# The first stage of a decoder block: small weights taken by halves, the first block of x ahead of the second, and one transfer moved to ScalarE's queue

## The chip, the cores and the metric

The kernel runs on one core of a Trainium2 chip. The metric is the device time of one execution in microseconds (us); the number given for a kernel is the median of its runs. A profile is one execution taken by the hardware profiler; its times count from the first instruction, and its span ends with the last.

Engines are named as the profile names them: PE (TensorE, matmuls), PEld (its weight loads), DVE (VectorE), ACT (ScalarE), POOL (GpSimd) and SP (SyncE, which here only issues DMAs). SPq and ACTq are the queues in which SP and ACT issue DMAs.

## The reference, cut to what matters

One layer on x of 512 tokens by 1024 channels, in float32. Only the first steps are touched by the change:

```python
hN = _rmsnorm(x, norm_g[l])          # x * rsqrt(mean(x*x) + eps) * g, per token
p = _split_in(hN @ w_in[l])          # one projection into all branches
...
vs = kvh(p["n_vs"])                  # selected and window values of the NSA branch
vw = kvh(p["n_vw"])
gates = jax.nn.sigmoid(p["n_g"] + b_nsa_gate[l])
...                                  # p["m_i"], p["m_f"]: input and forget gates of the mLSTM
```

Behind it come the two branches (a chunkwise mLSTM and a three-way sparse attention), their gates, two branch projections, a merge, an output projection, the residual and a last norm.

## The kernel before, in words

Every float32 product is made from two-part operands: a value is split into a high part (a rounded copy, written by ACT or POOL) and a low part (value minus high part, written by DVE), and a product is the sum of high x high, low x high and high x low. In the names, `h` at the end is a high part and `l` a low part: `hTh`, `hTl` for the normed and transposed x; `shi`, `slo` for the small weights; `wh`, `wl` for the others.

The first stage, which the change rewrites, takes the 512 tokens in four blocks of 128 (`xts[0]` to `xts[3]`, tile `xt`) and the 1024 channels in eight chunks `k` of 128. For each block `tb`:

- `stats(tb)`: ACT squares the block and sums it (`sq`; block 0 in two halves of 512 channels, the others in one piece), and POOL makes the factor `r` from the sum (`v`, then `r`).
- `normed(tb, hf)`: DVE multiplies one half of the channels by `r` and by the norm's weights, which lie in two PSUM banks.
- `turned(tb, hf, bank)`: four PE transposes into a PSUM bank; they need `ident`, the first 128 columns of `cst`.
- `high(tb, hf)` on ACT and `low(tb, hf)` on DVE write `hTh` and `hTl` from that bank; `whole(tb, hf)` on ACT keeps a plain copy in `gate` for later use.
- `some_of(tb, kind, ks)`: matmuls of 288 columns with the small weights (`w_small`: 288 columns of `w_in` for values and gates), `hh` = hTh x shi, `lh` = hTl x shi, `hl` = hTh x slo. A block needs 24 of them, 8 of each kind.
- `small_hi(k, eng)` and `small_lo(k)` split two chunks of the small weights, `raw` (tile `sraw`), into `shi` and `slo`. `raw` comes in two transfers of four chunks (576 KB each).
- `warm(n)`: n matmuls on zeros, which nothing uses.

All x blocks and both halves of `raw` come by SP's queue; the norm's weights and `ident` by ACT's.

In this stage ACT, DVE and PE run the instructions in the order in which the code names them (`tc.keep_in_program_order`), and POOL those under `keep(...)`. SP's DMAs are not kept: a scheduler places them. After `ordered.discard("pe")` the scheduler also places PE's work; there a stream of other weight products fills PE. A DMA on SP's queue also waits for an earlier one that used the same of eight semaphores (0 to 7).

After the first stage come the value, output-gate and gate-path products by a Strassen-like scheme (`winograd`), q and k, the attention, the mLSTM and the output projections. The change doesn't touch them.

Of the kernel before, what the change touches and what calls it, by code (L numbers as in the profile page):

```python
# [19 lines left out]
D = 1024  # L20
# [43 lines left out]
def build(  # L64
# [4 lines left out]
    nc = tc.nc  # L69
# [17 lines left out]
    keep = tc.keep_in_program_order  # L87
# [9 lines left out]
    def bank(tag, bufs):  # L97
        return psum.tile([128, 512], F32, name=tag, tag=tag, bufs=bufs)

    PP = lambda: bank("pp", 3)  # L100
# [4 lines left out]
    def f(ap):  # L105
        return ap.bitcast(F32)
# [181 lines left out]
    with tc.tile_pool(name="ph0", bufs=2, side="right") as p0, tc.tile_pool(  # L288
# [3 lines left out]
        xts = [p0.tile([128, D], F32, name="xt", tag="xt", bufs=4) for _ in range(NT)]  # L292
        raw = sp.tile([128, ND, SW], F32, name="sraw")

        grow = p0.tile([128, D], F32, name="grow", bufs=1)
        keep(nc.scalar.dma_start(grow[96:97, :], norm_g))
        act.preload_act_table_set("natural_log_exp_and_others")
        keep(nc.scalar.dma_start(cst[:, :CTRI], consts[:, :CTRI]))
        ordered.add("pe")
        zero = p0.tile([128, 384], F32R, name="zero", bufs=1)  # L300
# [4 lines left out]
        def warm(n):  # L305
            for _ in range(n):
                pe.matmul(idle[:, :256], zero[:, :128], zero[:, 128:], start=True, stop=True)

        warm(9)
        for hs in (slice(0, 512), slice(512, D)):  # L310
            nc.sync.dma_start(xts[0][:, hs], x[0, 0:128, hs])
        nc.sync.dma_start(xts[1], x[0, 128:256, :])
        for k in (0, 4):
            nc.sync.dma_start(raw[:, k : k + 4], w_small[:, k : k + 4])
        for tb in range(2, NT):
            nc.sync.dma_start(xts[tb], x[0, tb * 128 : (tb + 1) * 128, :])
        one = p0.tile([128, 128], F32, name="one", bufs=1)
# [10 lines left out]
        def small_hi(k, eng):  # L328
            ks = slice(k, k + 2)
            if eng == "a":  # L330
                A(shi[:, ks], raw[:, ks], AF.Copy)
            else:
                keep(pool.tensor_scalar(shi[:, ks], raw[:, ks], 1.0, 1.0, OP.mult, OP.mult))

        def small_lo(k):
            ks = slice(k, k + 2)
            dve.tensor_tensor(slo[:, ks], raw[:, ks], f(shi[:, ks]), OP.subtract)
# [4 lines left out]
        def squares(tb):  # L342
            sq = p0.tile([128, D], F32, name="sq", tag="sq", bufs=1)
            for n in range(1 if tb else 2):
                hs = slice(0, D) if tb else slice(n * 512, n * 512 + 512)
                part = ssq[:, NT * n + tb : NT * n + tb + 1]
                A(sq[:, hs], xts[tb][:, hs], AF.Square, accum_out=part, scale=D**-0.5)

        def factor(tb):
            v = p0.tile([128, 1], F32, name="v", tag="v", bufs=4)  # L350
            r = p0.tile([128, 1], F32, name="r", tag="r", bufs=4)
            rs.append(r)
            keep(pool.tensor_scalar(v, ssq[:, tb : tb + 1], EPS, None, OP.add))
            if tb == 0:
                keep(pool.tensor_tensor(v, v, ssq[:, NT : NT + 1], OP.add))
            keep(pool.tensor_tensor(r, v, mhalf[:, 0:1], OP.pow))

        def stats(tb):
            squares(tb)
            factor(tb)  # L360
# [16 lines left out]
        def normed(tb, hf):  # L377
            hs = slice(hf * 512, hf * 512 + 512)
            xv = xts[tb][:, hs]
            dve.scalar_tensor_tensor(xv, xv, rs[tb][:, 0:1], gB[hf], OP.mult, OP.mult)  # L380

        def turned(tb, hf, bank):
            for k in range(4):
                o = hf * 512 + k * 128
                pe.transpose(bank[:, k * 128 : (k + 1) * 128], xts[tb][:, o : o + 128], ident)
            banks[tb, hf] = bank.rearrange("p (k t) -> p k t", k=4)

        def high(tb, hf):
            A(hTh[:, hf * 4 : hf * 4 + 4, blk[tb]], banks[tb, hf], AF.Copy)

        def whole(tb, hf):
            q = gate[:, tb // 2 * 2 + hf].rearrange("p (k t) -> p k t", k=4)
            A(q[:, :, tb % 2 * 128 : tb % 2 * 128 + 128], banks[tb, hf], AF.Copy)

        def low(tb, hf):
            ks = slice(hf * 4, hf * 4 + 4)
            dve.tensor_tensor(
                hTl[:, ks, blk[tb]], banks[tb, hf], f(hTh[:, ks, blk[tb]]), OP.subtract
            )
# [3 lines left out]
        def some_of(tb, kind, ks, stop=False):  # L403
            ks = list(ks)
            start = tb not in sums
            if start:
                sums[tb] = PP()
            for k in ks:
                l = (hTl if kind == "lh" else hTh)[:, k, blk[tb]]
                r = (slo if kind == "hl" else shi)[:, k, :]  # L410
                pe.matmul(
                    sums[tb][:, :SW], l, r, start=start and k == ks[0], stop=stop and k == ks[-1]
                )

        lo4, hi4 = range(4), range(4, 8)
        stats(1)
        normed(0, 0)
        turned(0, 0, PT())
        warm(3)
        normed(0, 1)  # L420
        turned(0, 1, PT())
        small_hi(0, "p")
        high(0, 0)
        high(0, 1)
        small_hi(2, "a")
        warm(4)
        normed(1, 0)
        turned(1, 0, PP())
        some_of(0, "hh", lo4)
        normed(1, 1)  # L430
        turned(1, 1, idle)
        high(1, 0)
        small_hi(4, "a")
        high(1, 1)
        small_hi(6, "p")
        low(0, 0)
        small_lo(0)
        low(0, 1)
        small_lo(2)
        low(1, 0)  # L440
        low(1, 1)
        some_of(1, "hh", lo4)
        some_of(0, "lh", lo4)
        some_of(0, "hh", hi4)
        some_of(1, "hh", hi4)
        some_of(0, "lh", hi4)
        some_of(0, "hl", lo4)
        some_of(1, "hl", lo4)
        some_of(1, "lh", lo4)
        some_of(1, "lh", hi4)  # L450
        stats(2)
        whole(0, 0)
        whole(0, 1)
        stats(3)
        whole(1, 0)
        whole(1, 1)
        nc.sync.dma_start(bias, biases)
        vq = quarters(vview, ((0, 0), (1, 0)))
        normed(2, 0)
        turned(2, 0, PT())  # L460
        high(2, 0)
        small_lo(4)
        some_of(0, "hl", (4, 5))
        some_of(1, "hl", (4, 5))
        small_lo(6)
        some_of(0, "hl", (6, 7), stop=True)
        some_of(1, "hl", (6, 7), stop=True)
        normed(2, 1)
        turned(2, 1, PT())
        high(2, 1)  # L470
        some_of(2, "hh", lo4)
        normed(3, 0)
        turned(3, 0, idle)
        some_of(2, "hh", hi4)
        normed(3, 1)
        turned(3, 1, PS())
        low(2, 0)
        low(2, 1)
        evacuate(0, sums[0])
        for hf in range(2):  # L480
# [7 lines left out]
        for tb in (2, 3):  # L488
            if tb == 3:
                some_of(tb, "hh", lo4)  # L490
                some_of(tb, "hh", hi4)
            some_of(tb, "hl", lo4)
            some_of(tb, "hl", hi4)
            some_of(tb, "lh", lo4)
            some_of(tb, "lh", hi4, stop=True)
# [850 lines left out]
    for h in range(4):  # L1346
# [34 lines left out]
        for tb in range(NT):  # L1381
            po = PO() if tb == 2 else PT()
            for sb in range(tb + 1):
                a = KOFF[sb] + (tb - sb) * 128
                lh, ll = Sh[:, a : a + 128], Sl[:, a : a + 128]
# [307 lines left out]
```

## Time and profile before

| | us |
|---|---|
| median of 3 runs | 601.89 (601.44 to 602.06) |
| the profiled execution | 602.07 |
| its span, first to last instruction | 600.0 |
| PE busy | 590.8 (98%) |
| DVE, ACT, POOL busy | 484.9, 350.5, 81.1 |
| first stage on PE: start of the first transpose to the first matmul of the next stage | 7.52 to 26.19 |

PE is busy nearly throughout, so time is won or lost where PE stands still. A row of a timeline gives start, duration, engine, line, operation, output tile and input tile, shape, how often it stands in a row, and in brackets the idle time before it and what ended it. Line 80 is a helper through which all engines but POOL and SP record, so rows are told apart by their tiles.

### The profile page before, as it was taken

The numbers are of one execution on the slowest core, as the hardware profiler recorded it, in microseconds if no ns is written. First come the engines' busy times: TensorE is split into PE (matmuls) and PEld (weight loads), VectorE is DVE, ScalarE is ACT, GpSimd is POOL, SyncE is SP. The second block draws the span as 40 slices with busy tenths as digits, with TensorE's granted clock in tenths as the row PEclk, the third lists the DMA queues.
The fourth block names the chain that finished last, engine by engine and source line by source line (L and its number), as shares of the span: only waits on it lengthen the run. The fifth ranks groups of instructions, "written<-read, shape, count | busy, mean of one in ns | idle before, by whom it ended". The sixth has DMA issues, their size and how long they took to land.

```text
span 600.0 us, 8451 instructions
## 1 busy us (share of the span) xinstructions
PE 590.8 (98%) x2956; PEld 496.1 (83%) x2956; DVE 484.9 (81%) x901; ACT 350.5 (58%) x645; POOL 81.1 (14%) x136
## 2 busy tenths in 40 slices
PE   8999999999999999999999999999999999999995
PEld 6988888888888888888888888888888888888885
DVE  5899689597586889887977876889898979589975
ACT  6855546555447477566666765656566663424564
POOL 3000000000015013223323220001010101010121
PEclk9999999999999999999999999999999999999999
DMA  8946453502047663323133123422232236990733
GB/s 317 333 126 193 155 171 113 165 4 87 3 127 179 153 165 105 89 57 90 39 89 102 41 66 110 140 72 71 70 106 63 63 100 193 316 247 19 210 54 140
DMA packets 83573, 74.16 MB, mean 124 GB/s; under 512 B 3854, under 2 KB 65930, under 8 KB 83531
## 3 DMA queue, kind: packets, MB, share of 16 engines
q1 hardware_dynamic: 82232, 70.94, 39.3%
q0 software_dynamic: 1008, 2.36, 2.1%
q8 instruction: 23, 0.38, 0.3%
q10 hardware_dynamic: 290, 0.33, 0.2%
q14 instruction: 20, 0.16, 0.1%
HBM read 61.36 MB, written 8.45 MB: 116 GB/s over the span
## 4 chain that ended last, share of the span: by engine, by line
PE 79%; DVE 13%; ACT 3%; DMA 2%; issue 1%; POOL 1%; SPq 0%; POOLq 0%; ACTq 0%; DVEq 0%
PE pp L80 47%; PE ps L80 18%; PE pt L80 10%; DVE u L80 5%; PE po L80 4%; DVE wl L80 2%; ACT wh L80 1%; DMA xt<-x 1%; DVE qkl L80 1%; DVE num L80 1%; DVE xo L80 1%; POOL rho L1379 1%; ACT th L80 1%; DMA wr<-w_in 1%; ACT qkh L80 1%
## 5 line engine op out<-in xcount | busy, mean ns | idle before, releaser
L80 PE MATMUL pp<-hTl,wh 128*128 128x512 f32 x352 | 142.2, 404 | 0.0
L80 PE MATMUL pp<-hTh,wh 128*128 128x512 f32 x352 | 139.0, 395 | 0.0
L80 PE MATMUL pp<-hTh,wl 128*128 128x512 f32 x352 | 138.4, 393 | 0.0
L80 DVE TENSOR_TENSOR wl<-wr,wh 128x1024 fp32r<-128x1024 f32 x56 | 69.7, 1248 | 11.1 <-ACT wh L80 11.0
L80 PEld LDWEIGHTS pp<-hTh,wh 128*128 128x128 f32 x352 | 66.2, 188 | 12.8
L80 ACT ACTIVATE wh<-wr 128x1024 fp32r<-128x1024 f32 x56 | 58.3, 1058 | 30.3 <-PE pp L80 20.8
L80 PEld LDWEIGHTS pp<-hTh,wl 128*128 128x128 f32 x352 | 66.3, 188 | 10.6
L80 PEld LDWEIGHTS pp<-hTl,wh 128*128 128x128 f32 x352 | 66.3, 188 | 10.6
L80 ACT ACTIVATE P<-P,st 128x128 f32<-128x128 f32 (+3 forms) x64 | 35.7, 558 | 27.8 <-DVE st L80 27.7
L1123 POOL TENSOR_SCALAR P<-P,st 128x128 f32<-128x128 f32 (+3 forms) x56 | 37.8, 694 | 91.4 <-DVE st L80 59.4
L80 DVE TENSOR_TENSOR wl<-T,wh 128x1024 fp32r<-128x1024 f32 x28 | 34.1, 1223 | 14.5 <-ACT wh L80 14.4
L80 DVE TENSOR_TENSOR wl<-R,wh 128x1024 fp32r<-128x1024 f32 x28 | 33.8, 1220 | 10.2 <-ACT wh L80 10.1
L80 DVE TENSOR_TENSOR ptl<-pt,pth 128x512 fp32r<-128x512 f32 (+1 forms) x64 | 30.9, 485 | 11.3 <-ACT pth L80 10.6
L80 ACT ACTIVATE wh<-T 128x1024 fp32r<-128x1024 f32 x28 | 29.4, 1056 | 18.3 <-PE pp L80 11.0
L80 ACT ACTIVATE pth<-pt 128x512 fp32r<-128x512 f32 (+1 forms) x64 | 27.4, 428 | 20.4 <-PE pt L80 20.1
L80 ACT ACTIVATE wh<-R 128x1024 fp32r<-128x1024 f32 x28 | 29.1, 1056 | 12.4 <-PE pp L80 5.3
L80 DVE SCALAR_TENSOR_TENSOR u<-pp,prm,u 128x511 f32<-128x511 f32 (+2 forms) x48 | 35.7, 745 | 0.6 <-ACT u L80 0.2
L80 DVE CUSTOM_DVE_ANT_0 P<-ps,cst 128x128 f32<-128x128 f32 (+3 forms) x64 | 30.5, 483 | 6.6 <-PE ps L80 6.4
L80 PE MATMUL ps<-k,Th 128*128 128x256 f32 (+2 forms) x112 | 28.4, 336 | 0.0
L80 PE MATMUL pt<-cst,P 128*128 128x128 f32 x160 | 28.1, 272 | 0.0
L80 PEld LDWEIGHTS pt<-cst,P 128*128 128x128 f32 x160 | 20.8, 140 | 7.1 <-DVE ptl L80 0.3
L80 PE MATMUL pp<-yah,wh 128*128 128x512 f32 x64 | 25.0, 390 | 0.0
(355 smaller groups left out, 1360.1 us busy)
## 6 DMA issues: line engine op xcount, KB each, us to landing
wr<-w_in SPq DMA_DIRECT2D x44, 512.0 KB
R<-w_in SPq DMA_DIRECT2D x24, 512.0 KB
gD<-sg SPq DMA_DIRECT2D x16, 256.0 KB
s<-gD SPq DMA_DIRECT2D x16, 256.0 KB
wr<-w_branch_a SPq DMA_DIRECT2D x8, 512.0 KB
R<-w_out SPq DMA_DIRECT2D x8, 512.0 KB
vD<-cq SPq DMA_DIRECT2D x8, 256.0 KB
wr<-vD SPq DMA_DIRECT2D x4, 512.0 KB
```

Of the source, the lines that this page charges most:

```text
L80: ins = fn(*args, **kw)
L1123: pool.tensor_scalar(pj, pj, st[:, 2, j : j + 1], 1.0, OP.mult, OP.mult)
L1379: keep(pool.tensor_tensor(rho[:, b], v, mhalf[:, b], OP.pow))
```

## The change

Five things are altered, all in the first stage.

- DMAs: the second half of block 0 of x is issued by ACT, ahead of `ident`, no longer by SP. In the code SP's order is then: first half of block 0, first half of `raw`, block 1, second half of `raw`, blocks 2 and 3. It was: block 0 in two halves, block 1, `raw` in two halves, blocks 2 and 3.
- The high parts of the first half of `raw` are both POOL's, straight after block 0's factor; those of the second half are both ACT's.
- `stats(1)` moves behind `high(0, ...)`.
- Block 0's matmuls with the first half of the small weights, and its `hh` and `lh` ones with the second half, stand ahead of block 1's transposes.
- Blocks 1 and 2 take their matmuls in another order, and the `whole` copies and block 2's and 3's statistics stand elsewhere among them. `warm` goes from 7 to 8 matmuls behind the first transposes.

The number of all other instructions is the same.

```diff
@@ -295,6 +295,7 @@
         act.preload_act_table_set("natural_log_exp_and_others")
+        keep(nc.scalar.dma_start(xts[0][:, 512:], x[0, 0:128, 512:]))
         keep(nc.scalar.dma_start(cst[:, :CTRI], consts[:, :CTRI]))
...
         warm(9)
-        for hs in (slice(0, 512), slice(512, D)):
-            nc.sync.dma_start(xts[0][:, hs], x[0, 0:128, hs])
+        nc.sync.dma_start(xts[0][:, :512], x[0, 0:128, :512])
+        nc.sync.dma_start(raw[:, 0:4], w_small[:, 0:4])
         nc.sync.dma_start(xts[1], x[0, 128:256, :])
-        for k in (0, 4):
-            nc.sync.dma_start(raw[:, k : k + 4], w_small[:, k : k + 4])
+        nc.sync.dma_start(raw[:, 4:8], w_small[:, 4:8])
         for tb in range(2, NT):
             nc.sync.dma_start(xts[tb], x[0, tb * 128 : (tb + 1) * 128, :])
@@ -413,68 +413,71 @@
         lo4, hi4 = range(4), range(4, 8)
-        stats(1)
         normed(0, 0)
         turned(0, 0, PT())
         warm(3)
         normed(0, 1)
         turned(0, 1, PT())
         small_hi(0, "p")
+        small_hi(2, "p")
         high(0, 0)
         high(0, 1)
-        small_hi(2, "a")
-        warm(4)
+        stats(1)
+        small_lo(0)
+        low(0, 0)
+        small_lo(2)
+        low(0, 1)
+        warm(2)
+        second = PP()
+        some_of(0, "hh", lo4)
+        some_of(0, "hl", (0, 1))
+        some_of(0, "lh", lo4)
+        some_of(0, "hl", (2, 3))
+        small_hi(4, "a")
+        small_hi(6, "a")
+        warm(3)
+        for k in (4, 6):
+            some_of(0, "hh", (k, k + 1))
+            some_of(0, "lh", (k, k + 1))
         normed(1, 0)
-        turned(1, 0, PP())
-        some_of(0, "hh", lo4)
+        turned(1, 0, second)
         normed(1, 1)
+        whole(0, 0)
+        high(1, 0)
+        stats(2)
+        small_lo(4)
+        small_lo(6)
+        low(1, 0)
+        some_of(1, "hh", lo4)
         turned(1, 1, idle)
-        high(1, 0)
-        small_hi(4, "a")
         high(1, 1)
-        small_hi(6, "p")
-        low(0, 0)
-        small_lo(0)
-        low(0, 1)
-        small_lo(2)
-        low(1, 0)
+        whole(0, 1)
         low(1, 1)
-        some_of(1, "hh", lo4)
-        some_of(0, "lh", lo4)
-        some_of(0, "hh", hi4)
+        some_of(1, "hl", lo4)
+        some_of(0, "hl", hi4, stop=True)
+        stats(3)
         some_of(1, "hh", hi4)
-        some_of(0, "lh", hi4)
-        some_of(0, "hl", lo4)
-        some_of(1, "hl", lo4)
         some_of(1, "lh", lo4)
-        some_of(1, "lh", hi4)
-        stats(2)
-        whole(0, 0)
-        whole(0, 1)
-        stats(3)
+        some_of(1, "hl", hi4)
         whole(1, 0)
-        whole(1, 1)
         nc.sync.dma_start(bias, biases)
         vq = quarters(vview, ((0, 0), (1, 0)))
         normed(2, 0)
         turned(2, 0, PT())
         high(2, 0)
-        small_lo(4)
-        some_of(0, "hl", (4, 5))
-        some_of(1, "hl", (4, 5))
-        small_lo(6)
-        some_of(0, "hl", (6, 7), stop=True)
-        some_of(1, "hl", (6, 7), stop=True)
+        whole(1, 1)
+        some_of(1, "lh", hi4, stop=True)
         normed(2, 1)
         turned(2, 1, PT())
         high(2, 1)
         some_of(2, "hh", lo4)
         normed(3, 0)
         turned(3, 0, idle)
+        low(2, 0)
+        some_of(2, "hl", lo4)
         some_of(2, "hh", hi4)
         normed(3, 1)
         turned(3, 1, PS())
-        low(2, 0)
         low(2, 1)
         evacuate(0, sums[0])
@@ -488,8 +491,8 @@
             if tb == 3:
                 some_of(tb, "hh", lo4)
+                some_of(tb, "hl", lo4)
                 some_of(tb, "hh", hi4)
-            some_of(tb, "hl", lo4)
             some_of(tb, "hl", hi4)
```

How the built program's instructions stand, at the three places that matter most. First SP's queue at the start of the program, where x and the small weights are loaded (`xt` is x, `sraw` the small weights, `w_small` their source; the four transfers of whole or half x blocks are in the order of the blocks). Before:

```order
L311 DMA xt<-x 128x512 x2
L312 DMA xt<-x 128x1024
L314 DMA sraw<-w_small 128x1152 x2
L316 DMA xt<-x 128x1024 x2
L457 DMA bias<-biases 128x32
```

and now:

```order
L311 DMA xt<-x 128x512
L312 DMA sraw<-w_small 128x1152
L314 DMA sraw<-w_small 128x1152
L313 DMA xt<-x 128x1024
L316 DMA xt<-x 128x1024 x2
```

Both halves of `sraw` (lines 312 and 314) now stand ahead of block 1 (line 313), although the code names block 1 between them; the second 128x512 of x is gone from this queue.

Second ACT, from its first instruction to the high part of block 1's first half (`sq` is the squaring, 128x512 for block 0's halves and 128x1024 for a whole block; `hTh<-pt` is block 0, `hTh<-pp` block 1). Before:

```order
L296 DMA grow<-norm_g 1x1024
L80 ACT_TABLE_LOAD
L298 DMA cst<-consts 128x128
L80 ACTIVATE sq,ssq<-xt 128x512 x2
L80 ACTIVATE sq,ssq<-xt 128x1024
L80 ACTIVATE hTh<-pt 128x4x128 x2
L80 ACTIVATE shi<-sraw 128x576
L80 ACTIVATE hTh<-pp 128x4x128
```

and now:

```order
L296 DMA grow<-norm_g 1x1024
L80 ACT_TABLE_LOAD
L298 DMA xt<-x 128x512
L299 DMA cst<-consts 128x128
L80 ACTIVATE sq,ssq<-xt 128x512 x2
L80 ACTIVATE hTh<-pt 128x4x128 x2
L80 ACTIVATE sq,ssq<-xt 128x1024
L80 ACTIVATE shi<-sraw 128x576 x2
L80 ACTIVATE gate<-pt 128x4x128
L80 ACTIVATE hTh<-pp 128x4x128
```

Block 1's squaring went behind block 0's two high parts, and the two high parts of the small weights' second half stand behind that squaring.

Third PE, from block 0's second transposes to block 1's second (`pt_185` and `pt_179` are block 0's bank; `xt_117` is block 1; `pp_204`, now `pp_201`, collects block 0's sums and `pp_224`, now `pp_244`, block 1's; `po` from `zero` is `warm`). Before:

```order
L80 MATMUL pt_185<-cst_69,xt_116 128x128 x4
L80 MATMUL po_128<-zero_125 128x256 x4
L80 MATMUL pp_199<-cst_69,xt_117 128x128 x4
L80 MATMUL pp_204<-shi_157,hTh_77 128x288 x4
L80 MATMUL po_128<-cst_69,xt_117 128x128 x4
L80 MATMUL pp_224<-shi_157,hTh_77 128x288 x4
```

and now:

```order
L80 MATMUL pt_179<-cst_69,xt_116 128x128 x4
L80 MATMUL po_129<-zero_126 128x256 x2
L80 MATMUL pp_201<-shi_157,hTh_77 128x288 x4
L80 MATMUL pp_201<-slo_158,hTh_77 128x288 x2
L80 MATMUL pp_201<-shi_157,hTl_78 128x288 x4
L80 MATMUL pp_201<-slo_158,hTh_77 128x288 x2
L80 MATMUL po_129<-zero_126 128x256 x3
L80 MATMUL pp_201<-shi_157,hTh_77 128x288 x2
L80 MATMUL pp_201<-shi_157,hTl_78 128x288 x2
L80 MATMUL pp_201<-shi_157,hTh_77 128x288 x2
L80 MATMUL pp_201<-shi_157,hTl_78 128x288 x2
L80 MATMUL pp_200<-cst_69,xt_117 128x128 x4
L80 MATMUL pp_244<-shi_157,hTh_77 128x288 x4
```

Twenty of block 0's 24 matmuls now stand ahead of block 1's first transposes, where there were none, and nothing but block 1's own matmuls stands between block 1's two groups of transposes. Behind the first stage PE's instructions stand as before; on DVE a few small gate operations, and on SP one weight transfer, stand a few places elsewhere.

## The prediction

> **What bounds the kernel now.** I read the page first, then PE's waits, then the start of the chain of waits, and last the timelines of the first 27 us engine by engine. From the page, the span, PE's busy time and the chain's shares by engine:
>
> ```profile
> span 600.0 us, 8451 instructions
> PE 590.8 (98%) x2956; PEld 496.1 (83%) x2956; DVE 484.9 (81%) x901; ACT 350.5 (58%) x645; POOL 81.1 (14%) x136
> PE 79%; DVE 13%; ACT 3%; DMA 2%; issue 1%; POOL 1%; SPq 0%; POOLq 0%; ACTq 0%; DVEq 0%
> ```
>
> PE is the bound. Its waits over the whole span (who waited for whom, us in all, times, longest):
>
> ```profile
> PE pp L80 <- DVE xt L80: 1.3, 1, 1.3
> PE ps L80 <- PE pp L80: 0.2, 1, 0.2
> ```
>
> One wait of 1.3 us lies in the first stage, and after it PE is without work for 0.2 us until the tail. So whatever moves the end of PE's first stage should move the end of the program by as much: no later wait could absorb a loss. The chain of waits (start, duration, what) shows what sets that stage:
>
> ```profile
> 1.64 6.04 DMA xt<-x
> ...
> 7.76 1.15 ACT sq L80 x2
> 8.91 0.98 ACT hTh L80 x2
> ...
> 9.91 0.76 DVE xt L80
> 10.71 1.19 PE pp L80 x8
> ```
>
> Block 1's arrival (1.64 + 6.04 = 7.68), its squares, POOL's factor (at the place that the chain gives to `hTh`), its norm, its transposes. From 10.71 on PE works without a pause. PE's timeline, at the two edges of the stage:
>
> ```profile
> 7.52 0.63 PE L80 MATMUL pt<-cst,xt 128*128 128x128 f32 x4
> 7.91 0.60 PE L80 MATMUL po<-zero 128*128 128x256 f32 x3
> 8.35 0.60 PE L80 MATMUL pt<-cst,xt 128*128 128x128 f32 x4
> 8.70 0.72 PE L80 MATMUL po<-zero 128*128 128x256 f32 x4
> 10.71 0.66 PE L80 MATMUL pp<-cst,xt 128*128 128x128 f32 x4 [1.29 <-DVE xt L80]
> ...
> 20.42 0.60 PE L80 MATMUL ps<-cst,xt 128*128 128x128 f32 x4
> 20.77 1.31 PE L80 MATMUL pp<-slo,hTh 128*128 128x288 f32 x8
> 21.92 1.23 PE L80 MATMUL pp<-shi,hTl 128*128 128x288 f32 x8
> 22.99 1.23 PE L80 MATMUL pp<-shi,hTh 128*128 128x288 f32 x8
> ...
> 26.19 0.40 PE L80 MATMUL ps<-wh,hTh 128*128 128x512 f32 x1
> ```
>
> The stage ends at 26.19. Eight small matmuls take 22.99 - 21.92 = 1.07, so one 0.134; a group of four transposes costs 21.92 - 20.42 - 1.07 = 0.43.
>
> **The change, part by part.** The twenty matmuls that now stand ahead of block 1 (20 x 0.134 = 2.7 us) are to fill the gap of 1.29 and the fillers before it. But block 1 itself goes later, by two orders. I call S the start of block 1's squaring on ACT (7.76 before) and X that of the second half of block 0 (4.95 before). ACT's timeline:
>
> ```profile
> 3.54 0.63 ACT L80 ACTIVATE sq<-xt 128x512 f32<-128x512 f32 x1 [0.97 <-DMA xt<-x]
> 4.95 0.63 ACT L80 ACTIVATE sq<-xt 128x512 f32<-128x512 f32 x1 [0.69 <-DMA xt<-x]
> 7.76 1.06 ACT L80 ACTIVATE sq<-xt 128x1024 f32<-128x1024 f32 x1 [2.09 <-DMA xt<-x]
> 8.82 1.07 ACT L80 ACTIVATE hTh<-pt 128x512 fp32r<-128x512 f32 x2
> 9.77 0.68 ACT L80 ACTIVATE shi<-sraw 128x576 fp32r<-128x576 f32 x1
> 11.41 0.60 ACT L80 ACTIVATE hTh<-pp 128x512 fp32r<-128x512 f32 x1 [0.95 <-PE pp L80]
> ```
>
> *From S to the end of the stage.* Block 1's transposes follow S by 10.71 - 7.76 = 2.95. Its high part starts 11.41 - 10.71 = 0.70 later and takes 0.60, so at S + 4.3 PE gets block 1's first matmul. Before, four of block 0's matmuls covered that; now those have gone ahead, and PE stands from S + 3.4 to S + 4.3. What is left then: 4 matmuls of block 0 and 24 each of blocks 1 to 3, 76 x 0.134 = 10.15, and five groups of transposes, 5 x 0.43 = 2.15; so the end is S + 16.6. I followed ACT and DVE along with the durations of these rows and 0.70 to 0.75 for a half on DVE (15.09 below). The tightest place is block 2's first norm, which ends at about S + 7.55 for transposes that PE reaches at S + 7.9. So nothing more is added, and the stage breaks even at S = 26.19 - 16.6 = 9.6.
>
> *First bound on S, ACT's order.* The squaring stands behind block 0's two high parts. The rows of DVE and POOL:
>
> ```profile
> 6.09 0.57 POOL L356 TENSOR_TENSOR r<-v,prm 128x1 f32<-128x1 f32 x1
> 6.69 1.41 DVE L80 SCALAR_TENSOR_TENSOR xt<-xt,r,ps 128x512 f32<-128x512 f32 x2 [4.36 <-POOL r L356]
> 9.85 1.42 POOL L333 TENSOR_SCALAR shi<-sraw 128x576 fp32r<-128x576 f32 x2
> 15.09 0.75 DVE L80 SCALAR_TENSOR_TENSOR xt<-xt,r,ps 128x512 f32<-128x512 f32 x1
> ```
>
> X at 4.95 gave the factor at 6.66, the norms from 6.69, and the second transposes from 8.35 to 8.95: X + 4.0. The second high part then takes 0.60, so S is at least X + 4.6. The squaring at 7.76, which stood ahead of the high parts, is gone from before them. POOL's two high parts (1.42) now follow the factor, end at X + 3.2 and cover themselves behind the norms, if the first `sraw` half has landed; PE wants them at X + 3.9.
>
> *X itself.* The second half now comes by ACT's queue, issued where `ident` was (1.31), a little behind the first `sraw` half, which takes SP's second place:
>
> ```profile
> 0.73 0.87 SPq L311 DMA_DIRECT2D xt<-x  x2
> 1.31 0.36 ACTq L298 DMA_DIRECT2D cst<-consts  x1
> 1.64 0.43 SPq L312 DMA_DIRECT2D xt<-x  x1
> 7.69 0.90 SPq L268 DMA_DIRECT2D R<-w_in  x2
> 9.13 0.37 SPq L268 DMA_DIRECT2D R<-w_in  x1
> 10.54 0.37 SPq L139 DMA_DIRECT2D wr<-w_in  x1
> 11.83 3.02 SPq L139 DMA_DIRECT2D wr<-w_in  x1
> ```
>
> The last four rows are SP waiting for a semaphore of an earlier transfer, so they give landings: block 1 at 7.69, the `sraw` halves at 9.13 and 10.54, block 2 at 11.83. A `sraw` half (576 KB) so takes 1.44 and 1.41, a block (512 KB) 1.29. If the half block is served first, X stays at 4.95; if all of a `sraw` half goes before or between, X is 4.95 + 1.44 = 6.4. Its rival is in line earlier, so I take the far side, four fifths: 4.95 + 1.15 = 6.1, and S from this is 10.7.
>
> [...] No row here shows two large transfers on both queues at once.
>
> `ident` comes behind that half. It is 64 KB and is wanted at X + 2.57 (7.52 - 4.95), 1.8 `sraw` halves later, which covers it.
>
> *Second bound on S, block 1's landing.* It stood third on SP's queue; it now stands behind both `sraw` halves. The five transfers up to the second `sraw` half landed by 10.54. The same bytes with block 1 last land at 10.54 again, 2.85 later than block 1 did. There is room below: block 1 took 7.69 - 4.95 = 2.74 where block 2 took 1.29, so 1.45 of excess that may not come again. Bounds 9.1 and 10.6; I take 10.5, since the excess lies in the start, which remains.
>
> *The sum.* S is the later of 10.7 and 10.5: 10.7. The stage ends at 27.3, which is 1.1 later. PE's gap doesn't vanish; it moves: transposes of block 0 at 8.7 in place of 7.52, a wait for ACT's squaring, and 0.9 behind block 1's first transposes. The profiled execution goes from 602.07 (span 600.0) to 603.2 (601.1); that execution was 0.2 above the median, so 601.89 + 1.1 = **603.0 us**.
>
> **The rivals.** A measurement of this kernel can tell about 0.2%, 1.2 us, from no change.
>
> *A, the forecast*: both orders bite, X between 5.8 and 6.4, S 10.4 to 11.0, 602.7 to 603.3, and with 0.3 for small waits that I didn't find up to 603.6. Chance 0.50.
>
> *B, not slower*: the half block is served ahead of `sraw` (X = 4.95, S from ACT 9.55) and the excess is gone (block 1 at 9.1). S = 9.6 and the end stays: 601.9; with S at 10.1, 602.4. For it: its issue is only 0.1 later than before, and 1.45 of excess has no owner in the rows. Against: block 1 stands behind 1.1 MB more. Chance 0.23.
>
> *C, clearly slower*: the excess of 1.45 falls on block 0's second half, as it then shares the engines with the transfer that took block 1's place. X = 6.4 + 1.45 = 7.85, S = 12.45, end 29.05: +2.9, 604.8. It decides from X = 6.2 upwards (S = 10.8, +1.2). For it: the engines moved much less than later just then, in these stretches (stretch, its length, busy us and count of PE, PEld, DVE, ACT, POOL, then clock, DMA share, GB/s):
>
> ```profile
> 3.00:4.00 1.00, 1.00 (x4) 0.73 (x4) 0.00 (x0) 0.46 (x1) 0.00 (x0) 1.00 1.34 229
> ...
> 7.00:8.00 1.00, 1.00 (x11) 0.98 (x11) 1.00 (x2) 0.24 (x1) 0.00 (x0) 1.00 1.02 409
> ```
>
> Against: it struck block 1 while the half block landed. Chance 0.15.
>
> *D, PE's clock falls*: PE would stand longer between 7.7 and S + 4.3 = 15. Early matmuls of 256 columns ran slower than late ones:
>
> ```profile
> 1.31 2.29 PE L80 MATMUL po<-zero 128*128 128x256 f32 x9 [1.31 <-DVE zero L80]
> ```
>
> That is 0.25 each; later a fourth adds 0.72 - 0.60 = 0.12 (the rows at 7.91 and 8.70). If a slow stretch as long as the first (1.3 to about 7) came again inside the stage, half of 5.6 us is lost: +2.8 on top of 1.1, 605.8. Against: the fillers and the 20 matmuls still come in between. [...] Chance 0.05.
>
> *E, faster*: X can't be before about 4.2 (the first half's squaring starts at 3.54 and takes 0.63), so S is at least 8.8 and the stage's end at least 25.4: -0.8, 601.1. More than 0.2% would need a gain behind the stage, of which no row tells. Chance 0.07.
>
> **How the numbers follow.** The time is A's, 603.0. A's own range is 602.6 to 603.6. The range takes in B and most of C: 601.7 to 604.7; D, C's far end and half of E are left out, below 2 in 10. Slower by over 0.2% (over 603.1): half of A, C and D, 0.25 + 0.15 + 0.05 = 0.45. Within: the other half of A and B, 0.48. Faster: 0.07.
>
> **What would show it.** In the profile after: ACT's second `sq` of block 0 at 5.8 to 6.4 (B: 5.0; C: over 7); ACT's `sq` of block 1 at 10.4 to 11.0, ended by a high part or by its DMA; PE's first transposes of block 1 2.95 behind it, with 0.9 idle before the next `shi` matmul; the first `ps<-wh` matmul at 27.3. I am wrong in the step from stage to program if that matmul comes later and the span doesn't; wrong in the order if block 1 lands near 8; wrong in the count if S is as forecast and the stage ends more than 0.4 from S + 16.6.

## The result, and the profile after

The changed kernel took 604.63 us (median of 13 runs, 603.35 to 607.52), the kernel before 601.80 (13 runs, 601.36 to 602.15): 1.0059 times as long, 95% interval 1.0047 to 1.0070. The forecast was 603.0 with a range to 604.7. The time lies inside it, but it is slower beyond doubt, and of the loss of 2.83 only 1.1 was forecast.

The single runs show why. They fall into two groups that the mean granted clock of PE tells apart: seven at 603.4 to 604.6 with a clock of 0.996 to 0.999, and six at 606.1 to 607.5 with 0.992 to 0.994. The median is the highest run of the first group; had one more of the thirteen fallen into the second, it would stand at 606.07. The profiled execution (603.51, span 601.5) is of the first. From its page, span and busy time, and PE's waits over the whole span:

```profile
span 601.5 us, 8452 instructions
PE 591.6 (98%) x2957; PEld 496.4 (83%) x2957; DVE 484.9 (81%) x901; ACT 350.8 (58%) x645; POOL 80.5 (13%) x136
```

```profile
PE pt L80 <- DVE xt L80: 1.0, 1, 1.0
PE pp L80 <- ACT hTh L80: 0.7, 1, 0.7
PE ps L80 <- PE pp L80: 0.2, 1, 0.2
```

PE's one wait of 1.3 for block 1 has become two: 1.0 for block 0's transposes and 0.7 for block 1's high part. ACT's timeline:

```profile
3.44 0.63 ACT L80 ACTIVATE sq<-xt 128x512 f32<-128x512 f32 x1 [0.86 <-DMA xt<-x]
6.34 0.63 ACT L80 ACTIVATE sq<-xt 128x512 f32<-128x512 f32 x1 [2.17 <-DMA xt<-x]
10.38 0.60 ACT L80 ACTIVATE hTh<-pt 128x512 fp32r<-128x512 f32 x1 [0.20 <-PE pt L80]
10.87 1.06 ACT L80 ACTIVATE sq<-xt 128x1024 f32<-128x1024 f32 x1
```

X, the squaring of block 0's second half, went from 4.95 to 6.34 (forecast 6.1). S, that of block 1, went from 7.76 to 10.87 (forecast 10.7), and no DMA stands in its brackets: it followed the second high part, as ACT's order has it. Block 1 had landed well before: SP's instruction that waits for this landing goes on at 9.44 (forecast 10.5).

```profile
9.44 4.34 SPq L139 DMA_DIRECT2D wr<-w_in  x2
```

PE's timeline:

```profile
6.03 1.83 PE L80 MATMUL po<-zero 128*128 128x256 f32 x6
8.89 0.66 PE L80 MATMUL pt<-cst,xt 128*128 128x128 f32 x4 [1.03 <-DVE xt L80]
13.86 0.62 PE L80 MATMUL pp<-cst,xt 128*128 128x128 f32 x4
15.16 0.80 PE L80 MATMUL pp<-shi,hTh 128*128 128x288 f32 x4 [0.69 <-ACT hTh L80]
27.59 0.40 PE L80 MATMUL ps<-wh,hTh 128*128 128x512 f32 x1
```

Block 1's transposes come 13.86 - 10.87 = 2.99 behind S (forecast 2.95), and the stage ends at 27.59, S + 16.7 (forecast S + 16.6). It ends 1.40 later than before and the span is 1.5 longer, so nothing behind the stage absorbed it. The upper group is not in this profile; the experiments look for it.

### The profile page after: what moved, and what is told of

Same layout as the page of the kernel before. It is cut to its first block, busy times and chain, and to the rows that moved or that the text cites. A ratio compares the mean times of both kernels' runs of the same rounds, so it can differ in the third digit from the quotient of the medians.

```text
span 601.5 us, 8452 instructions
## 1 busy us (share of the span) xinstructions
PE 591.6 (98%) x2957; PEld 496.4 (83%) x2957; DVE 484.9 (81%) x901; ACT 350.8 (58%) x645; POOL 80.5 (13%) x136
## 4 chain that ended last, share of the span: by engine, by line
PE 83%; DVE 10%; ACT 3%; DMA 1%; issue 1%; POOL 1%; ACTq 0%; POOLq 0%; DVEq 0%
PE pp L80 49%; PE ps L80 19%; PE pt L80 11%; PE po L80 4%; DVE u L80 4%; DVE wl L80 2%; ACT wh L80 1%; DMA xt<-x 1%; DVE xo L80 1%; DMA wr<-w_in 1%; DVE num L80 1%; DVE qkl L80 1%; ACT th L80 1%; ACT qkh L80 1%; POOL rho L1382 0%
## 5 line engine op out<-in xcount | busy, mean ns | idle before, releaser
L80 ACT ACTIVATE wh<-T 128x1024 fp32r<-128x1024 f32 x28 | 29.4, 1057 | 18.4 <-PE pp L80 10.7
L80 DVE TENSOR_TENSOR ptl<-pt,pth 128x512 fp32r<-128x512 f32 (+1 forms) x64 | 30.9, 485 | 11.3 <-ACT pth L80 10.5
```

The costliest lines, as they stand in the source:

```text
L80: ins = fn(*args, **kw)
```

## The experiments

A kernel's runs are told apart below by their mean clock. In every profiled run the trace has the clock at one half for the last 1.4 to 4.5 us, which alone gives a mean of 0.996 to 0.999; 3.41 us at one half inside the first stage take off another 0.003 (1.7 us of a span of 601). So a run at 0.995 or less lost the clock for some us, and one at 0.996 may have lost it too.

| kernel | runs | of them at 0.995 or less | median of the others |
|---|---|---|---|
| changed (three series: 13, 5, 6) | 24 | 11 (median 606.76) | 603.51 |
| changed, with more fillers (three series: 5, 7, 8) | 20 | 0 | 603.61 |
| changed, half back on SP's queue | 11 | 0 | 602.54 |
| changed, half first on ACT's queue | 5 | 0 | 604.20 |
| the same, squaring between the high parts | 5 | 0 | 603.56 |
| changed, half back, squaring between | 11 | 0 | 602.62 |
| changed, SP's order as written | 7 | 3 (604.6 to 605.3) | 603.27 |
| before, half on ACT's queue | 12 | 2 (603.95, 606.17) | 602.07 |
| before, without seven fillers | 8 | 3 (603.6 to 603.8) | 601.23 |
| before (three series beside these) | 59 | 1 (603.51) | 601.8 |

**The changed kernel again.** Nothing edited. On record:

> The changed kernel once more, for the two groups into which its runs fell (603.4 to 604.6 at a mean granted clock of 0.996 to 0.999, and 606.1 to 607.5 at 0.992 to 0.994). Theory 1, PE's clock falls again inside the first stage: about half of the runs above 606 with a mean clock under 0.995; if the profiled run is one of them, its matmuls of 288 columns stand about 0.24 apart for some 5 us of the first 20 us, in place of 0.134. Theory 2, the DMAs of the start land up to 3 us later in some runs: a run above 606 shows the second half of block 0 at 9 or later and matmuls at 0.134 throughout.

Five runs: 606.88, 605.19, 603.19, 604.02, 603.51. The profiled one is that of 606.88, clock 0.992. Its ACT and PE rows:

```profile
8.11 0.63 ACT L80 ACTIVATE sq<-xt 128x512 f32<-128x512 f32 x1 [3.97 <-DMA xt<-x]
13.79 1.05 ACT L80 ACTIVATE sq<-xt 128x1024 f32<-128x1024 f32 x1
```

```profile
5.65 1.28 PE L80 MATMUL po<-zero 128*128 128x256 f32 x6
10.65 1.12 PE L80 MATMUL pt<-cst,xt 128*128 128x128 f32 x4 [3.72 <-DVE xt L80]
13.49 1.16 PE L80 MATMUL pp<-shi,hTh 128*128 128x288 f32 x4
31.14 0.40 PE L80 MATMUL ps<-wh,hTh 128*128 128x512 f32 x1
```

And in four consecutive stretches of this run PE's busy us with the count of its matmuls, granted clock, DMA share, GB/s:

```profile
5.28:8.69 3.41, 1.66 (x9) 1.00 1.02 392
8.69:12.10 3.41, 1.45 (x7) 0.50 1.03 405
12.10:15.52 3.42, 3.42 (x17) 0.50 1.05 388
15.52:18.93 3.41, 2.72 (x21) 1.00 1.15 322
```

Both theories are right in part. The half landed 1.77 later than in the first profile (8.11 against 6.34), and the clock was at one half from 8.69 to 15.52: four matmuls of 288 took 1.16 in place of 0.69, and they stood 0.24 apart. From S the stage then needs 31.14 - 13.79 = 17.35 in place of 16.7, and S is X + 5.7 in place of X + 4.5. So the 3.55 that this run lost against the first profile are 1.77 for the late half and 1.8 for the clock. The expectation of either cause alone was too narrow, and one run in five came above 606 in place of half.

Two things in these traces say more. The half's landing is marked sixteen times in each. In the first profile the fifteenth mark stands at 6.23 and the last at 6.32; here the fifteenth stands at 6.38 and the last at 8.09. So the late half is one late mark of sixteen. And PE's gap ahead of block 0's transposes has two ends: the fillers before it ended at 6.03 + 1.83 = 7.86 in the first profile and at 5.65 + 1.28 = 6.93 here. The clock first rose at 7.18 there and at 5.28 here, and the four matmuls on the norm's weights and the six fillers took 3.62 and 1.83 there, 2.81 and 1.28 here. Of the 2.69 by which the gap grew (1.03 to 3.72), 1.76 lies at its end and comes from the late half, and 0.93 lies at its start and comes from the fillers.

**More fillers.** Where PE stood still it now multiplies zeros; the stage's work is the same.

```diff
-        warm(6)          # ahead of block 0's transposes
+        warm(14)
...
-        warm(3)          # behind block 0's first twelve matmuls
+        warm(5)
...
         turned(1, 0, second)
+        warm(6)
```

> The changed kernel with 16 more filler matmuls on zeros in its three gaps: 8 ahead of block 0's first transposes, 2 behind block 0's first twelve matmuls, 6 behind block 1's first transposes (0.12 us each, less than each gap). Theory 1 (the clock falls because PE stands still): the upper group is gone or rare, the mean clock 0.996 or more in every run, the median 603.3 to 603.8. Theory 2 (late DMAs): both groups stay, the median 604 to 606.

Five runs at 603.19 to 604.44, median 603.52, none at 0.995 or less. A second version has 18 in place of the 14:

> The changed kernel with 20 more filler matmuls: 12 ahead of block 0's first transposes, 2 behind block 0's first twelve matmuls, 6 behind block 1's first transposes. It parts the late landing from the clock. If a late half (squaring at 8 in place of 6.3) costs 1.8 by itself and the clock's fall the rest: the typical runs at 603.2 to 603.8, late ones at 604.8 to 605.5, none above 606, mean clock 0.996 or more throughout. If fillers don't hold the clock: some runs at 606 to 607.5 at 0.992 to 0.994, as without them.

Seven runs at 603.19 to 604.22, median 603.57. To see whether late halves still come, that version ran again beside the changed kernel:

> The changed kernel unaltered, beside the next, for the share of slow runs. If slow runs are a late half and a fallen clock together: about a third above 605, those with a mean clock of 0.996 or less.

> The changed kernel with 20 more filler matmuls (12, 2 and 6 in its three gaps), once more. If the fillers hold the clock and the half is at times late all the same: none above 606, some at 604.8 to 605.5 at a mean clock of 0.996 or more, most at 603.2 to 604.0. If the clock's fall alone makes the slow runs: all at 603.2 to 604.4.

The changed kernel: 603.39 to 606.76, four of six at 0.995 or less. With the fillers: eight runs, none at 0.995 or less; five at 603.0 to 603.9, two at 604.8 and 605.0 with a clock of 0.999, and one at 606.11 with 0.996. So the fillers hold the clock (0 of 20 runs at 0.995 or less against 11 of 24), and they give the median back from 604.6 to 603.6. The runs at 604.8 and 605.0 have lost 1.2 to 1.5 at full clock, somewhat less than the 1.77 of a late half; no trace of such a run is at hand, so that cause is argued. The run at 606.11 goes against the expectation (none above 606) and is not explained: at 0.996 it may have lost the clock after all.

**The half back on SP's queue.**

```diff
-        keep(nc.scalar.dma_start(xts[0][:, 512:], x[0, 0:128, 512:]))
...
         nc.sync.dma_start(xts[0][:, :512], x[0, 0:128, :512])
+        nc.sync.dma_start(xts[0][:, 512:], x[0, 0:128, 512:])
         nc.sync.dma_start(raw[:, 0:4], w_small[:, 0:4])
```

> The changed kernel with the second half of block 0 back on SP's queue, second, ahead of the small weights; the built order then is x half, x half, first small weights, block 1, second small weights. Theory of the forecast (time = S + 16.6): the squaring of that half starts at 4.9 to 5.1 in place of 6.34, that of block 1 at 9.5 to 9.7 in place of 10.87 (ACT's order decides, block 1 lands before 9), the first matmul of the next stage at 26.1 to 26.4; the group without a clock loss at 601.8 to 602.3. A loss of clock in some runs is still possible, since the gap behind block 1's transposes stays. Rival: the move is hidden behind block 1, and the time stays at 603.5 or more.

```profile
5.09 0.63 ACT L80 ACTIVATE sq<-xt 128x512 f32<-128x512 f32 x1 [0.99 <-DMA xt<-x]
9.63 1.05 ACT L80 ACTIVATE sq<-xt 128x1024 f32<-128x1024 f32 x1
```

```profile
26.34 0.40 PE L80 MATMUL ps<-wh,hTh 128*128 128x512 f32 x1
```

X 5.09, S 9.63, end S + 16.7: the rule holds at another S. The runs lie at 601.89 to 603.41, median 602.54, 1.0017 (1.0009 to 1.0026) of the kernel before, and none of eleven lost the clock. So of the 1.7 that the changed kernel loses at full clock (603.51 against 601.81), 1.0 is the queue and 0.7 the rest of the change. In this build block 1 also stands between the two halves of the small weights again; the run with SP's order as written, below, shows no gain from that alone. Expected were 601.8 to 602.3, and 602.54 came, 0.24 above that; these runs don't show where the 0.24 lies.

**The queue alone, in the kernel before.** The second half goes to ACT's queue, SP's two x transfers are named ahead of it so that block 1 stays second on SP's queue.

```diff
+        nc.sync.dma_start(xts[0][:, :512], x[0, 0:128, :512])
+        nc.sync.dma_start(xts[1], x[0, 128:256, :])
         keep(nc.scalar.dma_start(grow[96:97, :], norm_g))
         act.preload_act_table_set("natural_log_exp_and_others")
+        keep(nc.scalar.dma_start(xts[0][:, 512:], x[0, 0:128, 512:]))
...
-        for hs in (slice(0, 512), slice(512, D)):
-            nc.sync.dma_start(xts[0][:, hs], x[0, 0:128, hs])
-        nc.sync.dma_start(xts[1], x[0, 128:256, :])
```

> The kernel before with one part of the change: the second half of block 0 by ACT's queue behind the norm's weights and ahead of ident; SP's order is first half, block 1, both small weights, blocks 2 and 3. Theory (the move delays that half, because it then shares the transfer engines with what SP sends meanwhile): its squaring starts at 6.0 to 6.5 in place of 4.95, in some runs at 8. Block 1's squaring stays at 7.7 to 8.0, since block 1 lands as before, so block 1's transposes stay at 10.7 to 11.2 and most runs at 601.8 to 602.4; runs with the half at 8 lie at 603 to 605. Rival (the queue itself delays nothing; it was the place behind the small weights): squaring of the half at 4.9 to 5.2, all runs at 601.4 to 602.2.

```profile
6.54 0.63 ACT L80 ACTIVATE sq<-xt 128x512 f32<-128x512 f32 x1 [2.38 <-DMA xt<-x]
7.29 1.06 ACT L80 ACTIVATE sq<-xt 128x1024 f32<-128x1024 f32 x1
```

```profile
5.71:9.12 3.41, 1.46 (x9) 1.00 1.01 394
9.12:12.54 3.42, 3.42 (x16) 0.50 1.04 406
```

X is 6.54 here, 6.34 in the changed kernel: the half is late with block 1 as its neighbour as it was with the small weights. What the two have in common is a large transfer next on SP's queue; in the changed kernel's trace ACT's queue moved 0.26 MB between 3.5 and 6.05 us while SP's moved 0.63 MB. That the half is late because both queues move data at once is my reading. Block 1 covers the delay (most runs at 602.05, 0.25 over the kernel before), but the clock doesn't bear it: the profiled run (603.95) lost it from 9.12 to 12.54. Two runs at 603.50 and 603.51, with 0.996 and 0.997, are not explained.

**The half first in line on ACT's queue.**

```diff
+        keep(nc.scalar.dma_start(xts[0][:, 512:], x[0, 0:128, 512:]))
         keep(nc.scalar.dma_start(grow[96:97, :], norm_g))
         act.preload_act_table_set("natural_log_exp_and_others")
-        keep(nc.scalar.dma_start(xts[0][:, 512:], x[0, 0:128, 512:]))
```

> The changed kernel with the second half of block 0 as the first transfer of ACT's queue, ahead of the norm's weights (issued at 0.73, beside SP's first half), so that it is in line ahead of the small weights; the built order on SP is then as written, block 1 between the halves of the small weights. Theory (what delays the half is what stands in line ahead of it, not the queue): its squaring at 4.4 to 5.1, block 1's at 9.0 to 9.7, the next stage's first matmul at 25.8 to 26.3, runs at 601.6 to 602.6, no upper group. Rival (ACT's queue gets a smaller share whenever SP's is full): squaring at 6 or later and runs at 603 or more.

```profile
4.71 0.61 ACT L80 ACTIVATE sq<-xt 128x512 f32<-128x512 f32 x1
```

```profile
4.10 3.75 PE L80 MATMUL ps<-grow,one 97*128 97x512 f32 x4 [0.50 <-DMA grow<-norm_g]
6.86 2.27 PE L80 MATMUL po<-zero 128*128 128x256 f32 x6
8.93 1.05 PE L80 MATMUL pt<-cst,xt 128*128 128x128 f32 x4
9.63 0.99 PE L80 MATMUL po<-zero 128*128 128x256 f32 x3
```

The half did come early, at 4.71, so the theory of the line (4.4 to 5.1) holds here against its rival (6 or later). The time didn't follow: 604.20. The norm's weights, 4 KB behind the half, now landed later, and PE's matmuls on them started at 4.10 in place of 3.40. In this trace the clock first rises at 10.88 (at 7.18 in the changed kernel's). Ahead of that the six fillers took 2.27 in place of 1.83 and held PE until 8.9, so block 0's transposes waited for PE itself, and they too ran slowly (1.05 for four in place of 0.66, then 0.99 for three fillers in place of 0.61). A new wait, not foreseen; why the clock rose so late is not shown.

**The squaring between block 0's high parts,** on top of that kernel; the first four transfers on SP's queue are also held in the order in which that kernel's build had them.

```diff
         high(0, 0)
-        high(0, 1)
         stats(1)
+        high(0, 1)
```

> As the one before, with block 1's squaring between block 0's two high parts on ACT in place of behind both. Theory (time = S + 16.6, and ACT's order sets S): S falls by about 0.6 to 8.7 or 9.0 (block 1's landing then decides), the next stage's first matmul at 25.3 to 25.7, 601.2 to 601.9, which is 0.4 to 0.7 below the kernel before it in this list. Rival (the second high part, 1 us later, delays block 0's last matmuls by as much): no gain.

603.56, 0.64 below the last kernel. The step is of the size expected, but not by the rule: in the profiles S fell by 1.02 (11.78 to 10.76) and the next stage's first matmul by 0.56 (28.49 to 27.93). The absolute numbers expected (601.2 to 601.9) came out wrong with those of the last kernel. The same edit with the half back on SP's queue should have been level with the kernel before:

> The changed kernel with the second half of block 0 back on SP's queue, second, and block 1's squaring between block 0's two high parts. Theory (time = S + 16.6): S at 8.8 to 9.0 (its landing decides), the next stage's first matmul at 25.5 to 25.9, runs at 601.6 to 602.2: level with the kernel before, 0.4 to 0.8 under the one with the half back alone (602.54). Rival: other waits make up for it, 602.4 or more.

```profile
9.03 1.05 ACT L80 ACTIVATE sq<-xt 128x1024 f32<-128x1024 f32 x1
```

```profile
12.30 0.43 PE L80 MATMUL pp<-shi,hTl 128*128 128x288 f32 x2
12.57 0.60 PE L80 MATMUL pp<-cst,xt 128*128 128x128 f32 x4
26.27 0.40 PE L80 MATMUL ps<-wh,hTh 128*128 128x512 f32 x1
```

A miss: 602.62. S is 9.03 as expected, but the transposes of block 1 stand at S + 3.54, without an idle gap ahead of them: PE reaches them only when it is through block 0's twenty matmuls. S + 16.6 holds while the norm is later than PE; below S of about 9.6 PE's own queue is the bound, and an earlier squaring brings nothing. No version of the changed kernel in this list beats the kernel before.

**SP's order as written.** The first four transfers on SP's queue are kept in the order of the code.

```diff
-        nc.sync.dma_start(xts[0][:, :512], x[0, 0:128, :512])
+        keep(nc.sync.dma_start(xts[0][:, :512], x[0, 0:128, :512]))
...                      # the same for raw, block 1, raw
```

> The changed kernel with SP's transfers held in the order of the code: block 1 between the halves of the small weights (the small bias, 16 KB, slips ahead of block 1). Theory (block 1's landing doesn't bind; ACT's order after the late half does): block 1 lands about 1.2 earlier, its squaring still follows block 0's second high part at 10.6 to 11.0, and the typical runs stay at 603.3 to 604.0. Rival (block 1 behind both small weights is the loss): its squaring at 9.5 or earlier and runs at 602.5 or less.

Runs at full clock: 603.12 to 603.73, as without the edit. Block 1's landing, which the forecast had nearly level with ACT's order (10.5 against 10.7), doesn't bind; it came at 9.44 at the latest in the first profile, so there was room. In the profiled run, which lost the clock, the squaring of block 1 has no DMA ahead of it either:

```profile
6.85 0.63 ACT L80 ACTIVATE sq<-xt 128x512 f32<-128x512 f32 x1 [2.68 <-DMA xt<-x]
12.54 1.05 ACT L80 ACTIVATE sq<-xt 128x1024 f32<-128x1024 f32 x1
```

**The kernel before without its seven fillers** behind block 0's transposes.

```diff
         turned(0, 0, PT())
-        warm(3)
...
         small_hi(2, "a")
-        warm(4)
```

> The kernel before without the seven filler matmuls behind block 0's transposes, so PE does only eight transposes between 7.6 and 10.7. Theory 1: some runs lose the clock, 2 to 4 us longer at a mean clock under 0.996; the others stay at 601.9. Theory 2: all runs at 601.4 to 602.2, clock 0.997 or more.

Three of eight runs at 603.6 to 603.8 with 0.994 and 0.995, the others at 601.1 to 602.1. Expected were 2 to 4 us more, and 1.7 to 1.9 came. The profiled one lost the clock:

```profile
7.35:10.76 3.41, 1.46 (x13) 1.00 1.02 411
10.76:14.18 3.42, 3.10 (x14) 0.50 1.05 396
```

So the kernel before owes its clock (lost in 1 of 59 runs) to its fillers, and the same fault can be made from the other side. The five runs that kept the clock have a median of 601.23 against 601.8, but they spread over 601.1 to 602.1 as the kernel before does, so a gain from leaving the fillers out isn't shown.

**When the clock falls.** Each stretch above begins and ends at a change of the clock or 3.41 us from one. First the stretch ahead of the fall with SP's order as written, then the stretch of the same kind from kernels whose profiled run kept the clock (before; changed; changed again; half back):

```profile
5.94:9.35 3.41, 1.31 (x8) 1.00 1.01 410
...
6.82:10.23 3.41, 2.60 (x22) 1.00 1.02 410
...
7.18:10.59 3.41, 2.38 (x21) 1.00 1.03 420
...
6.38:9.79 3.41, 2.13 (x16) 1.00 1.03 410
...
5.64:9.05 3.41, 2.88 (x20) 1.00 1.02 393
```

PE was busy for 2.13 to 2.88 of 3.41 us where the clock stayed, and for 1.31 (SP's order as written), 1.46, 1.46 and 1.66 where it fell at the stretch's end. Four falls and four that held, with no overlap; in none of these stretches was PE busy for between 1.66 and 2.13. In each of these stretches the idle time is one piece, 0.53 to 1.28 us where the clock stayed and 1.75 to 2.10 where it fell. So these runs can't tell whether the busy share of a stretch decides or the length of one idle piece in it. The end of a stretch can part a gap: the kernel before stood for 1.29 from 9.42 to 10.71, of which 0.81 lie ahead of 10.23. Where the stretches lie differs from run to run (the clock first rose at 4.85 to 7.50 in twelve of the profiled runs and at 10.06 and 10.88 in the other two).

## Why the prediction was right and wrong

- *From the stage to the program*: right. 1.40 at the stage's end, 1.5 in the span, 603.51 against 602.07 in the profiled executions (forecast 603.2).
- *S + 16.6*: right, at 10.87 and 9.63 (S + 16.7 both times), with a limit that I hadn't named: below 9.6 PE's own queue bounds block 1's transposes (3.54 behind S in place of 2.95).
- *First bound on S, X + 4.6*: right in the typical run (10.87 - 6.34 = 4.5).
- *X = 6.1*: near in the typical runs, 6.2 to 6.4 in the profiles of the changed kernel, with more fillers or without. It was taken as one number. Rival C, a half that comes 1.5 to 2 later, is not an alternative to A but a part of the same kernel's runs: 8.11 in one.
- *Second bound on S, block 1 at 10.5*: too late by 1.1, since block 1 was there when SP went on at 9.44, so most of the 1.45 of excess did not come again (that part of rival B was right). The bound doesn't act: holding SP's order as written, which takes a small-weight transfer out of block 1's way, left the full-clock runs at 603.1 to 603.7.
- *Rival D, PE's clock*: this is the step that failed. The sum has no term for the clock, and the chance of a fall was put at 0.05; it came in 11 of 24 runs. The reason given, that the fillers and the twenty matmuls come in between, leaves out the gap ahead of block 0's transposes and how much it varies. That gap was 1.0 to 1.3 in the profiles of the changed kernel that kept the clock, and 3.72 in the one that lost it, by a late half and by fillers that ended early. In the four traces with a fall, 1.75 to 2.10 of idle time lay in the 3.41 ahead of it. The price was mis-sized too: a fall by itself costs 1.8 in the run of 606.88 (6.83 us at half clock) and 1.2 with SP's order as written (3.41 us; S stands at X + 5.7 in place of X + 4.5 and the rest is as without a fall), against 2.8 forecast. That the groups lie 606.76 - 603.51 = 3.25 apart comes near the 2.8 by luck: in the run of 606.88 the late half is half of it. It is luck as well that the median lies inside the range, from which rival D had been left out.
- *The size at full clock*: with the clock held, 603.51 to 603.61 against 601.81 is 0.28 to 0.30%, against 0.18% forecast (1.1). Of the difference of 0.6, 0.34 is that the two profiles differ by 1.44 rather than 1.1, and 0.26 that the profiled execution of before lies above the median of its runs.

## What to carry to other kernels

A transfer that the first work waits for should stand ahead of the bulk in line; putting it on a second queue beside the bulk made it 1.25 us later (X 5.09 to 6.34), and the stage's end moved by as much (26.34 to 27.59). Where PE waits for something of uncertain arrival, reckon the gap with the latest arrival, hold it against the idle time that lay ahead of a fall of the clock (here 1.75 to 2.10 us in a stretch of 3.41), and keep fillers there: here they cost at most 0.1 in the median at full clock and were worth 1 us in the median of all runs. When runs of one kernel spread by more than those of its neighbour, sort them by granted clock before explaining the median.

## What the runs showed of the hardware

In the four profiled runs that lost PE's clock inside the first stage it fell at 8.69, 9.12, 9.35 and 10.76, each time 3.41 us after it had first risen (5.28, 5.71, 5.94 and 7.35), and it was at one half for 3.41, in one run for 6.83. In the 3.41 ahead of the fall PE was busy for 1.31 to 1.66 us, so it had not stood still throughout; with 2.13 to 2.88 in the stretch of the same kind the clock stayed.

The same 256 KB of x landed in time for a squaring at 4.71 (first in line on ACT's queue), 5.09 (second on SP's) and 6.2 to 6.9, once 8.11, on ACT's queue beside larger transfers. In the run at 8.11 the last of the sixteen marks of its landing came 1.71 behind the fifteenth; why it came so late stays open.
